# Weight loads and their two splitting operations at the highest scheduler priority, in a two-block transformer kernel on one core

## The chip, the cores and the metric

The kernel runs on one core of one Trainium2 chip. The metric is the device time of one execution in microseconds; the figure quoted is the median of several executions, and the profile is one further execution with the hardware profiler on.

## The reference

The input x has 256 tokens of 1024 features, in float32. Two blocks follow each other.

```python
def hybrid_layer(x, ...):                      # first block, two layers, l = 0 and 1
    x = x + 0.5 * swiglu(rmsnorm(x, ffn1_norm), gate, up, down)      # d_ff 2816
    h = rmsnorm(x, mix_norm) @ w_in
    o_a = chunk_relpos_attention(...)          # 6 heads, relative-position bias
    o_b = dsa_attention(...)                   # 5 heads, 64 keys chosen by an index score
    o_c = mla_attention(...)                   # 5 heads, low-rank queries and keys
    x = x + concatenate([o_a, o_b, o_c]) @ w_out
    x = x + 0.5 * swiglu(rmsnorm(x, ffn2_norm), gate, up, down)

def second_block(x, c, ctx, ...):              # one layer
    mod = silu(c) @ w_mod + b_mod              # and the same for the context
    h, hc = modulated norms of x and of ctx (256 context tokens)
    y = token_mixer(h, hc, ...)                # mLSTM and gated linear attention, both directions
    x = x + g1 * y
    x = x + g2 * peer_ffn(h2, ...)             # product-key experts, 8 heads, 16 of 16384 each
    return rms_norm(x, norm_f_g)
```

## The kernel before

All activations are kept feature-major: 128 partitions, 8 feature tiles, 256 tokens (`T`). The large products have float32 precision out of reduced-precision matmuls: each weight piece and each activation is split into a high part H (a copy in the reduced type) and a low part L (the float32 value minus H), and every product is three matmuls, H by xH, H by xL and L by xH (`mm3`, L251 to L258; `mm3t`, L260 to L267, has the weights as the moving operand). A weight is therefore ready for TensorE only when it has been loaded, copied on ScalarE (ACT) and subtracted on VectorE (DVE).

Class `W` (L205) does this in `load` (L211). A piece is up to 1024 columns of a weight. For each piece SyncE (SP) issues one DMA into a buffer `raw` (L215; five buffers), ACT copies it to `wH` (L218; three buffers), and DVE subtracts it into `wL` (L219; three buffers). Some other transfers use the same five `raw` buffers (the modulation weights at L714). `wchunk` (L248) loads a whole weight.

The order of each engine's instructions is set by a tile scheduler, which takes ready operations by priority; without other marks the priority is the order in which the program calls them. Engines run their queues in order.

The program (`run`, L1488): constants and x are loaded first, with the first four pieces of 512 columns of the first feed-forward weight (`self.ahead`) called between the four DMAs of x (L1502 to L1505). Then, for l = 0 and 1: `ffn` (L384) for ffn1, `mixer` (L494), and `ffn` for ffn2. `ffn` first calls `split_scaled` (L353: xH on ACT at L360, xL on DVE at L361) and `stats` (L284; squares on ACT at L294 and L298, sums on DVE at L299 and L300, the root by L277 to L281, the spread over partitions by two transposes at L313 and a copy `rb` on ACT at L315). Its loop over j runs 22 times: 48 matmuls into a bank `mm` (two banks while these layers run), the bank scaled by `rb` into `gu` on DVE (L400), silu on ACT (L401), the product (L403) and its split (L404, L405). During ffn2 of l = 0 and ffn1 of l = 1 the modulation of block two is computed beside (`modulation`, L714 and L717). ffn2 of l = 1 has the second block's context side beside it (`context`, L1418), with gates through exponentials on ACT (L862, L866) and on DVE (L881, L917). `mixer` projects its heads with `pair` and token-major values with `tokmajor` (the weights `win_bv` and `win_av`), and rotates with `rope` (DVE at L434, L435, L437). `latents` (L1448) then does the token mixer for x, with gates again (L863, L881, L917, L922), the running state C (L1071, L1077), the division of x by its norm (L748, eight tiles), and small matmuls on the gates' results at L954 and L962. The sums of squares before the last block's expert part are `sums` (squares on ACT, additions on DVE at L331 and L332, matmuls at L339), followed by the root and transposes at L348 (`spread`). `peer` (L1212) has the experts.

Of the kernel before, what the change touches and what calls it, by code (L numbers as in the profile page):

```python
# [9 lines left out]
F32 = mybir.dt.float32  # L10
# [5 lines left out]
AF = mybir.ActivationFunctionType  # L16
OP = mybir.AluOpType
# [187 lines left out]
class W:  # L205
# [4 lines left out]
    def load(self, pieces=None):  # L210
        k = self.k  # L211
        for o in range(self.cut * len(self.H), self.cols, self.cut)[:pieces]:
            n = min(self.cut, self.cols - o)
            raw = k.wp.tile([128, 1024], F32, name="raw", tag="raw", bufs=5)
            k.nc.sync.dma_start(raw[:, :n], self.src[:, o:o + n])  # L215
            H = k.wp.tile([128, 1024], F32R, name="wH", tag="wH", bufs=3)
            L = k.wp.tile([128, 1024], F32R, name="wL", tag="wL", bufs=3)
            k.nc.scalar.activation(H[:, :n], raw[:, :n], AF.Copy)  # L218
            k.nc.vector.tensor_tensor(L[:, :n], raw[:, :n], H[:, :n].bitcast(F32), op=OP.subtract)  # L219
            self.H.append(H)  # L220
            self.L.append(L)
        return self
# [1346 lines left out]
```

## Time and profile before

| what | value |
|---|---|
| median of 3 runs | 2152.27 us (2152.04 to 2153.51) |
| the profiled execution | 2156.47 us |
| its span, first to last instruction | 2154.5 us |
| mean granted TensorE clock, share of full | 0.991 |
| TensorE (PE) busy | 2096.3 us, 97% |
| weight loads of TensorE (PEld) busy | 2035.3 us, 94% |
| DVE busy | 1587.1 us, 74% |
| ACT busy | 1160.5 us, 54% |
| bytes moved by DMA | 385.35 MB, 179 GB/s |

The engines work side by side, so their busy times do not add up; an engine with 97% has 3% of the span in which it could still be better fed. A row of the timeline has a start, a duration, an engine, a line of the program and the operation; what stands in brackets is the idle time of the engine just before it, and what ended it. The view of waits sums such idle time by the line that waited and the operation it waited for. The clock column of a stretch is the share of full TensorE clock granted in it.

### The profile page before, as it was taken

To read this page: it belongs to the slowest core of one execution; us is meant where nothing else is said; L and a number is where in the kernel's file an instruction comes from. 1 tells how busy PE (TensorE), PEld (TensorE's weight loads), DVE (VectorE), ACT (ScalarE), POOL (GpSimd) and SP (SyncE) were. 2 spreads that over 40 slices of the span, in tenths; PEclk is the share of its full clock that TensorE was granted. 3 is DMA by queue.
4 is the path that set the end of the run, shared out by engine and by line. 5 is a ranking of instruction groups with operands and counts; after the bars stand their busy time and mean duration, and the time that the engine had idled before them with its cause. 6 is when DMAs were issued, how large, how long until landed. Compare 5 with 4: busy or idle time off the path is not lost. (4 is left out here: it accounts for less than half of the span.)

```text
span 2154.5 us, 43075 instructions
## 1 busy us (share of the span) xinstructions
PE 2096.3 (97%) x17204; PEld 2035.3 (94%) x17204; DVE 1587.1 (74%) x3211; ACT 1160.5 (54%) x2011; POOL 17.4 (1%) x35
## 2 busy tenths in 40 slices
PE   8999999999999999999999998999999999999997
PEld 8999989999999998998998798999999999999997
DVE  6776977786787697777758858888888885555555
ACT  5544465444444445547446555544588884444444
POOL 0000000000000000000000000000000000000000
PEclk9999999999999999999999999999999999999999
DMA  6666535667787753455464334555544445555553
GB/s 231 218 202 191 156 99 175 207 211 229 248 270 247 234 159 106 151 170 169 157 185 138 127 118 144 188 179 177 181 154 159 159 157 192 190 189 188 187 189 125
DMA packets 115112, 385.35 MB, mean 179 GB/s; under 512 B 12768, under 2 KB 13920, under 8 KB 114784
## 3 DMA queue, kind: packets, MB, share of 16 engines
q1 hardware_dynamic: 114912, 382.61, 54.7%
q8 instruction: 135, 2.21, 0.4%
q14 instruction: 65, 0.53, 0.1%
HBM read 380.46 MB, written 2.10 MB: 178 GB/s over the span
## 5 line engine op out<-in xcount | busy, mean ns | idle before, releaser
L219 DVE TENSOR_TENSOR wL<-raw,wH 128x1024 fp32r<-128x1024 f32 (+3 forms) x716 | 811.8, 1137 | 353.1 <-ACT wH L218 350.4
L218 ACT ACTIVATE wH<-raw 128x1024 fp32r<-128x1024 f32 (+3 forms) x716 | 705.8, 989 | 631.2 <-PE mm L257 439.0
L256 PE MATMUL mm<-xH,wH 128*128 128x256 f32 x2952 | 840.0, 285 | 9.5 <-ACT xH L360 6.4
L258 PE MATMUL mm<-xH,wL 128*128 128x256 f32 x2952 | 837.0, 284 | 8.0 <-DVE wL L219 7.9
L257 PE MATMUL mm<-xL,wH 128*128 128x256 f32 x2952 | 835.4, 283 | 1.3 <-DVE xL L361 0.8
L256 PEld LDWEIGHTS mm<-xH,wH 128*128 128x128 f32 x2952 | 559.7, 190 | 13.3 <-ACT xH L360 6.4
L258 PEld LDWEIGHTS mm<-xH,wL 128*128 128x128 f32 x2952 | 559.9, 190 | 12.3 <-DVE wL L219 11.0
L257 PEld LDWEIGHTS mm<-xL,wH 128*128 128x128 f32 x2952 | 559.9, 190 | 4.4 <-DVE xL L361 2.0
L256 PE MATMUL mm<-hl,wH 128*128 128x256 f32 x1024 | 285.8, 279 | 0.0
L257 PE MATMUL mm<-hl,wH 128*128 128x256 f32 x1024 | 285.8, 279 | 0.0
L258 PE MATMUL mm<-hl,wL 128*128 128x256 f32 x1024 | 285.8, 279 | 0.0
L258 PE MATMUL mm<-hH,wL 128*128 128x256 f32 x704 | 198.0, 281 | 6.2 <-DVE wL L219 6.1
L256 PE MATMUL mm<-hH,wH 128*128 128x256 f32 x704 | 196.6, 279 | 0.0
L257 PE MATMUL mm<-hL,wH 128*128 128x256 f32 x704 | 196.6, 279 | 0.0
L256 PEld LDWEIGHTS mm<-hl,wH 128*128 128x128 f32 x1024 | 192.4, 188 | 0.0
L258 PEld LDWEIGHTS mm<-hl,wL 128*128 128x128 f32 x1024 | 192.4, 188 | 0.0
L257 PEld LDWEIGHTS mm<-hl,wH 128*128 128x128 f32 x1024 | 192.4, 188 | 0.0
L258 PEld LDWEIGHTS mm<-hH,wL 128*128 128x128 f32 x704 | 132.1, 188 | 8.6 <-DVE wL L219 8.4
L717 DVE SCALAR_TENSOR_TENSOR prod<-raw,cv 128x1024 f32<-128x1024 f32 x64 | 78.3, 1223 | 73.8 <-DMA raw<-wmod 72.7
L257 PEld LDWEIGHTS mm<-hL,wH 128*128 128x128 f32 x704 | 132.1, 188 | 0.0
L256 PEld LDWEIGHTS mm<-hH,wH 128*128 128x128 f32 x704 | 132.0, 188 | 0.0
L401 ACT ACTIVATE gu<-gu 128x256 f32<-128x256 f32 x88 | 36.4, 414 | 105.4 <-DVE gu L400 105.1
(461 smaller groups left out, 2539.3 us busy)
## 6 DMA issues: line engine op xcount, KB each, us to landing
raw<-ffn_gu SPq DMA_DIRECT2D x174, 512.0 KB, 4.6
raw<-ut SPq DMA_DIRECT2D x128, 512.0 KB, 4.0
raw<-vt SPq DMA_DIRECT2D x128, 512.0 KB, 4.5
raw<-win SPq DMA_DIRECT2D x58, 512.0 KB, 4.4
raw<-wmod SPq DMA_DIRECT2D x48, 512.0 KB, 4.4
raw<-ffn_d SPq DMA_DIRECT2D x64, 384.0 KB, 3.2
raw<-ffn_d SPq DMA_DIRECT2D x64, 320.0 KB, 3.2
raw<-wout SPq DMA_DIRECT2D x24, 512.0 KB, 3.7
```

What stands on the lines that cost most here:

```text
L218: k.nc.scalar.activation(H[:, :n], raw[:, :n], AF.Copy)
L219: k.nc.vector.tensor_tensor(L[:, :n], raw[:, :n], H[:, :n].bitcast(F32), op=OP.subtract)
L256: mm(out, H, xH[:, k], start=first, stop=False, skip_group_check=skip)
L257: mm(out, H, xL[:, k], start=False, stop=False, skip_group_check=skip)
L258: mm(out, L, xH[:, k], start=False, stop=last, skip_group_check=skip)
L401: nc.scalar.activation(gu[:, 0], gu[:, 0], AF.Silu)
L717: nc.vector.scalar_tensor_tensor(out, raw, 1.0, cv[:, D * i:D * i + D], op0=OP.mult, op1=OP.mult, accum_out=self.mod[:, j, i:i + 1])
```

## The change

The three operations of a piece (the DMA, ACT's copy, DVE's subtraction) are put in a `high_priority()` block of the scheduler; the two tiles H and L are now named before the DMA. `high_priority()` makes the scheduler prefer these operations, on each engine, over every other one that is ready. No operation is added or removed, and buffers stay as they are. All lines behind the edit have a number that is higher by two.

```diff
             raw = k.wp.tile([128, 1024], F32, name="raw", tag="raw", bufs=5)
-            k.nc.sync.dma_start(raw[:, :n], self.src[:, o:o + n])
             H = k.wp.tile([128, 1024], F32R, name="wH", tag="wH", bufs=3)
             L = k.wp.tile([128, 1024], F32R, name="wL", tag="wL", bufs=3)
-            k.nc.scalar.activation(H[:, :n], raw[:, :n], AF.Copy)
-            k.nc.vector.tensor_tensor(L[:, :n], raw[:, :n], H[:, :n].bitcast(F32), op=OP.subtract)
+
+            with k.tc.high_priority():
+                k.nc.sync.dma_start(raw[:, :n], self.src[:, o:o + n])
+                k.nc.scalar.activation(H[:, :n], raw[:, :n], AF.Copy)
+                k.nc.vector.tensor_tensor(L[:, :n], raw[:, :n], H[:, :n].bitcast(F32), op=OP.subtract)
             self.H.append(H)
             self.L.append(L)
```

Four places show what this does to the queues. The first is the start of SP's queue, which issues the loads: `raw` are weight pieces, `cst_76` constants, `x` the input. Before:

```order
L380 DMA cst_76<-cst 128x384
L215 DMA raw<-ffn_gu 128x512
L1505 DMA x<-xT 128x512 x2
L215 DMA raw<-ffn_gu 128x512
L1505 DMA x<-xT 128x512 x2
L215 DMA raw<-ffn_gu 128x512 x2
```

and now:

```order
L219 DMA raw<-ffn_gu 128x512 x4
L219 DMA raw<-ffn_gu 128x1024
L382 DMA cst_76<-cst 128x384
L219 DMA raw<-ffn_gu 128x1024 x3
L1507 DMA x<-xT 128x512 x4
```

The four DMAs of x moved from between the first pieces to behind the eighth piece; of the last three pieces ahead of them, each needs a `raw` buffer that one of the first three pieces gives back.

The second is ACT's queue at the start, from the first piece to the first `rb`. Before:

```order
L218 ACTIVATE wH<-raw 128x512
L360 ACTIVATE xH<-x,cst_76 128x256 x2
L218 ACTIVATE wH<-raw 128x512
L360 ACTIVATE xH<-x,cst_76 128x256 x6
L294 ACTIVATE sq<-x 128x512
L298 ACTIVATE sq<-x 128x512 x2
L218 ACTIVATE wH<-raw 128x512
L298 ACTIVATE sq<-x 128x512
L218 ACTIVATE wH<-raw 128x512
L218 ACTIVATE wH<-raw 128x1024 x4
L315 ACTIVATE rb<-at 128x256
```

and now:

```order
L220 ACTIVATE wH<-raw 128x512 x3
L362 ACTIVATE xH<-x,cst_76 128x256 x8
L296 ACTIVATE sq<-x 128x512
L220 ACTIVATE wH<-raw 128x512
L300 ACTIVATE sq<-x 128x512 x2
L220 ACTIVATE wH<-raw 128x1024
L300 ACTIVATE sq<-x 128x512
L220 ACTIVATE wH<-raw 128x1024 x4
L317 ACTIVATE rb<-at 128x256
```

The copy of the ninth piece, which stood behind `rb`, now stands ahead of it, as the last of the nine.

The third is DVE's queue in `latents`, from the division of x (L748 before, L750 now) to the gates (`la`, `lf`). Before:

```order
L748 SCALAR_TENSOR_TENSOR x<-x,cst_76,rb 128x256 x8
L1071 TENSOR_SCALAR wv<-mv,col_12316 128x129 x3
...
L1077 SCALAR_TENSOR_TENSOR C<-C,abc_12314,c 128x129 x2
L863 TENSOR_SCALAR la<-at,cst_11262 128x256 x2
L872 MEMSET mv 128x8
L219 TENSOR_TENSOR wL<-raw,wH 128x1024
L863 TENSOR_SCALAR la<-at,cst_11262 128x256
L219 TENSOR_TENSOR wL<-raw,wH 128x1024 x2
L881 SCALAR_TENSOR_TENSOR lf<-G,E 64x256
```

and now:

```order
L750 SCALAR_TENSOR_TENSOR x<-x,cst_76,rb 128x256 x4
L221 TENSOR_TENSOR wL<-raw,wH 128x1024
L750 SCALAR_TENSOR_TENSOR x<-x,cst_76,rb 128x256 x4
L221 TENSOR_TENSOR wL<-raw,wH 128x1024 x2
L1079 SCALAR_TENSOR_TENSOR C<-C,abc_12314,c 128x129
L1073 TENSOR_SCALAR wv<-mv,col_12316 128x129 x3
...
L865 TENSOR_SCALAR la<-at,cst_11262 128x256
L221 TENSOR_TENSOR wL<-raw,wH 128x1024
L883 SCALAR_TENSOR_TENSOR lf<-G,E 64x256
L919 TENSOR_TENSOR la<-la,E 128x1024
```

The three subtractions that stood behind all of the state's updates now stand inside and right behind the division of x.

The fourth is DVE's queue at the sums of squares ahead of the expert part (`x` is the last update of the residual, `sq` the squares). Before:

```order
L331 TENSOR_TENSOR sq<-sq 128x256
L1482 SCALAR_TENSOR_TENSOR x<-c,mod,x 128x256 x2
L332 TENSOR_TENSOR sq<-sq 128x256
L219 TENSOR_TENSOR wL<-raw,wH 128x1024
L757 TENSOR_SCALAR rm<-at 128x2
```

and now:

```order
L1484 SCALAR_TENSOR_TENSOR x<-c,mod,x 128x256 x2
L333 TENSOR_TENSOR sq<-sq 128x256
L221 TENSOR_TENSOR wL<-raw,wH 128x1024
L333 TENSOR_TENSOR sq<-sq 128x256
L334 TENSOR_TENSOR sq<-sq 128x256
```

The subtraction moved from behind the last addition to ahead of the last two, and two additions moved behind the last update of x.

## Rows read from the trace of the kernel before

**Rows 1.** The page, busy time of the engines.

```profile
PE 2096.3 (97%) x17204; PEld 2035.3 (94%) x17204; DVE 1587.1 (74%) x3211; ACT 1160.5 (54%) x2011; POOL 17.4 (1%) x35
```

**Rows 2.** Waits of PE, whole span: us in total, times, longest.

```profile
PE mm L258 <- DVE wL L219: 14.0, 21, 2.3
...
PE mm L266 <- DVE wL L219: 6.1, 3, 3.4
...
PE c L266 <- DVE wL L219: 1.5, 1, 1.5
...
PE c L258 <- DVE wL L219: 0.7, 1, 0.7
```

**Rows 3.** Timeline of PE, matmuls 1 to 48: start, us, operation, [idle before].

```profile
6.37 0.58 PE L256 MATMUL mm<-xH,wH 128*128 128x256 f32 x1 [6.37 <-ACT xH L360]
...
11.84 0.41 PE L258 MATMUL mm<-xH,wL 128*128 128x256 f32 x1
12.05 0.41 PE L256 MATMUL mm<-xH,wH 128*128 128x256 f32 x1
...
16.91 0.28 PE L257 MATMUL mm<-xL,wH 128*128 128x256 f32 x1
17.02 0.28 PE L258 MATMUL mm<-xH,wL 128*128 128x256 f32 x1
```

**Rows 4.** Waits of PE from 400 to 760 us.

```profile
PE mm L258 <- DVE wL L219: 8.9, 17, 1.4
```

**Rows 5.** Timeline of PE in the first mixer, at the values' weight.

```profile
218.34 0.42 PE L266 MATMUL mm<-wL,xH 128*128 128x328 f32 x1 [1.39 <-DVE wL L219]
```

**Rows 6.** Waits of PE from 960 to 1000 us.

```profile
PE mm L258 <- DVE wL L219: 2.3, 1, 2.3
...
PE mm L256 <- ACT wH L218: 0.9, 1, 0.9
```

**Rows 7.** Timeline of PE in latents: the two long waits, and the gates' matmul.

```profile
1175.36 0.39 PE L258 MATMUL mm<-xH,wL 128*128 128x256 f32 x1 [1.80 <-DVE wL L219]
...
1189.05 0.50 PE L266 MATMUL mm<-wL,xH 128*128 128x512 f32 x1 [3.37 <-DVE wL L219]
...
1201.51 0.48 PE L954 MATMUL at<-dg,ones 64*128 64x128 f32 x2
```

**Rows 8.** Stretches of 2 us: busy us of PE, PEld, DVE, ACT, POOL; granted clock; DMA.

```profile
982.00:984.00 2.00, 0.51 (x5) 0.30 (x3) 1.94 (x5) 1.99 (x3) 0.00 (x0) 1.00 0.07 27
984.00:986.00 2.00, 1.17 (x7) 1.17 (x8) 2.00 (x4) 1.13 (x3) 0.00 (x0) 0.81 0.10 25
986.00:988.00 2.00, 2.00 (x11) 2.00 (x11) 1.83 (x7) 1.21 (x2) 0.00 (x0) 0.50 0.63 231
988.00:990.00 2.00, 2.00 (x15) 1.91 (x15) 2.00 (x5) 0.81 (x1) 0.00 (x0) 0.84 0.06 14
```

**Rows 9.** DMA, 0 to 40 us: rate per us, and issues (KB each, median us to landing).

```profile
GB/s 0 60 254 129 367 358 215 238 334 383 420 418 426 250 41 266 262 340 274 274 328 258 246 311 209 250 94 213 262 156 283 152 115 279 139 90 295 160 164 307
...
x<-xT SPq DMA_DIRECT2D x4, 256.0 KB, 5.1
```

**Rows 10.** Timeline of ACT at the start.

```profile
5.81 0.91 ACT L360 ACTIVATE xH<-x,cst 128x256 fp32r<-128x256 f32 x2
...
20.06 1.06 ACT L218 ACTIVATE wH<-raw 128x1024 fp32r<-128x1024 f32 x1 [1.77 <-PE mm L257]
```

**Rows 11.** Timeline of DVE around the first use of rb.

```profile
21.33 1.22 DVE L219 TENSOR_TENSOR wL<-raw,wH 128x1024 fp32r<-128x1024 f32 x1
22.47 0.68 DVE L400 TENSOR_TENSOR gu<-mm,rb 128x512 f32<-128x512 f32 x1
```

**Rows 12.** Stretch of 40 us in the second mixer, columns as in rows 8.

```profile
760.00:800.00 40.00, 38.44 (x284) 35.56 (x283) 37.92 (x101) 20.57 (x33) 1.30 (x1) 1.00 0.54 168
```

**Rows 13.** Timeline of DVE in latents, at the end of the gates' chain.

```profile
1195.25 0.41 DVE L948 TENSOR_TENSOR gd<-b,mu 64x256 f32<-64x256 f32 x1
```

**Rows 14.** Timeline of PE at the sums of squares.

```profile
1322.12 1.75 PE L339 MATMUL at<-ones,sq 128*128 128x1 f32 x12 [1.72 <-DVE sq L332]
```

## Prediction

> **What bounds the kernel now.** First the busy times [rows 1]: TensorE (PE) works 2096.3 us of a span of 2154.5, so all its idle time is 58.2 us. DVE, which makes every wL, is at 74%, so only the order of its work, not its amount, can starve PE. Then PE's waits [rows 2]: what it waits for the second splitting operation sums to 14.0 + 6.1 + 1.5 + 0.7 = 22.3 us. That is the most that a better order of weights can win directly. The single longest wait, 6.37 us, is for the first xH, and that is no weight [rows 3]: before the first matmul PE needs a piece and x. So the same priority that can shorten 22.3 us can lengthen 6.37.
>
> Where the 22.3 us lie decides. 8.9 of them fall between 400 and 760 us [rows 4], where the modulation of the second block shares `raw`, and DVE, with the feed-forward layers; the new order of all queues there is the old one, so I count nothing. The others: 1.39 us at `win_bv` in the first mixer [rows 5] and as much in the second, 2.3 + 1.5 + 0.7 and 0.9 for a wH around 980 us [rows 2, 6], and 1.80 + 3.37 in `latents` [rows 7].
>
> An idle PE also costs clock. In the 2.0 us in which PE was busy 0.51, the granted clock still stood at 1.00; then it read 0.81, 0.50 and 0.84 in the next three stretches [rows 8], between the levels 2.4 and 1.2 GHz. Lost there: 0.19 x 1.17 + 0.50 x 2 + 0.16 x 2, about 1.5 us. I take 1.7 us as the price of one idle stretch of about 2 us, between 0 (a short idle) and 3.6 us (4 us of idle and of half clock twice as long).
>
> **The start: a cost.** x's DMAs took 5.1 us from issue to landing when one or two pieces stood ahead [rows 9]; now x lies behind eight pieces and the constants. Ahead of the end of x's first quarter stand 4 x 256 + 4 x 512 + 192 + 256 KB = 3520 KB, 3.60 MB. The first 12 us of the rate row move 3.18 MB, the first 13 move 3.60 [rows 9]. So x's first quarter lands near 13.0 us where xH started at 5.81 [rows 10]. The first matmul came 0.56 us behind that, at 6.37 [rows 3]; it now comes near 13.65. If the queue never falls below some 400 KB per us it is 12.6; if the last three pieces wait longer for their `raw` buffers, 14.6.
>
> By the Trainium skill, DMA: Bandwidth & Descriptors, section Queues, rings and completion order, each engine takes the descriptors of a queue in ring order, so x would not overtake the pieces. The same page puts the HBM side at about 358 GB/s and the port side at 435, an estimate of 8.3 to 10.1 us for 3.60 MB; the rate row reaches 426 but averages less, so the row's 13 us are kept.
>
> From there PE runs without waits for pieces, all of which are ready. The matmuls started 0.21 us apart until 12.05, and 0.11 to 0.12 us apart at 16.91 [rows 3]: the lower level of the clock for about 6 us, or 28 matmuls. With the same here, 48 matmuls take 28 x 0.214 + 20 x 0.118 = 8.4 us, to 22.0 us; before, the 48th started at 17.02 and ended its share at 17.1. **Cost 4.9 us**, from 3.6 to 6.0.
>
> Then a new wait. ACT's copy of the ninth piece now stands ahead of `rb`, and it needs a wH buffer that the sixth piece holds until the 96th matmul is done (the old row shows such a copy waiting 1.77 us for PE [rows 10]). Behind it comes the subtraction of the ninth piece on DVE, and behind that the first `gu`, which frees the bank that matmul 97 needs, since there are two. From the end of matmul 96: copy 1.06 [rows 10], subtraction 1.22, gu 0.68 [rows 11], together 2.96, of which some 0.25 is overlap. **Cost 2.7 us**, from 0 (if a wH buffer is free sooner) to 4.0 (with the transposes ahead). After such an idle stretch the clock falls: **1.7 us**, 0 to 3.6. Together the start costs 9.3 us, 5 to 12.
>
> **The mixers: a small gain.** At `win_bv` the subtraction moves ahead of the rotation's DVE work, and the waits of 1.39 go: **2.8 us won** [rows 5], 0 to 2.8. What was covering it, the masked copies behind the rotation, now end later by two subtractions, about 1.6 us, against the 1.4 that PE gains; the matmuls on them had no wait, so this is about even. In the head part the values' matmuls come earlier as filler, and fewer are left between the later heads, while DVE there is the busier engine (37.92 of 40 us in the second mixer [rows 12]). I charge **1 us** for both mixers; bounds 0 to 5.
>
> **960 to 1000 us: a gain.** The subtractions move ahead of the context's splits and products. Of 2.3 + 0.9 + 1.5 + 0.7 = 5.4 us about 1.3 stay, since one subtraction still stands behind `lf` (L881) and `la` (L917), which wait for ACT. So 4.1 direct, and of the two falls of the clock behind these waits a bit more than one, 1.9. **6.0 won**, 3 to 8.
>
> **Latents: a gain given back in part.** Three subtractions move from behind the state's updates to inside the division of x, and later ones ahead of the scans: the waits of 1.80 and 3.37 go [rows 7], and two falls of the clock with them, 3.4. Against that the gates' chain (`lf`, scans, `mu`, `it`) stands behind five subtractions of 1.22, some on its path. The matmul at L954 that takes its result came at 1201.51 [rows 7]; the last DVE step of the chain ended at 1195.66 [rows 13], and with ACT's exponential behind it the inputs were ready some 4 us before. PE now reaches it 8.6 us earlier and 47 matmuls (7 us) later in its order, but the chain is some 6 us later: a new wait of about 3 us, and a fall of 1.7 behind it. **3.9 won**, 1 to 8.
>
> **The sums of squares: a cost.** PE waits 1.72 us there for the last addition [rows 14]. One subtraction (1.22) and two more additions (0.33 each as they follow each other) now stand between the last update of x and that addition: **1.9 us**, 0 to 2.5. PE has nothing else to do there.
>
> In the expert part PE has no wait that a weight ends, and the swaps there are of single operations: 0, from nothing won to 2 lost.
>
> **Sum:** 9.3 - 2.8 + 1.0 - 6.0 - 3.9 + 1.9 = -0.5 us. The profiled execution took 2156.47 us, 2.0 more than its span and 4.2 more than the median of the runs; the terms are differences against that span, so I set the sum against the median: 2152.27 - 0.5, about **2152 us**. A measurement of this kernel can tell about 0.2%, 4.3 us, from no change; this is inside.
>
> **Rivals.** *Weights win* (faster): the start costs 6.6, because the first `gu` is not held up, and latents and the stretch around 980 give 7 and 7.5. Then 6.6 - 2.8 + 1 - 7.5 - 7 + 1.9 = -7.8, 2144.5 us. For it: ACT is at 54% and DVE has slack in these stretches. Against it: two queues show the ninth piece ahead of the first `rb` and `gu`.
>
> *The gates' chain and the heads are starved* (slower): each subtraction that overtakes a step of a chain on which PE waits next costs its 1.22 us. It decides once five or more stand on the path to L954 and two or more on that of each mixer's last heads: latents then win nothing (3.9 lost), each mixer costs 2.4 (4.8 less the 1 counted), so -0.5 + 3.9 + 3.8 = +7.2, 2159.5 us. For it: DVE at 37.92 of 40 us [rows 12]. Against it: in these stretches PE's own matmuls are still long enough to hide several microseconds.
>
> *The order hardly changes where it counts*: in the layers between 400 and 760 us this is so already; if also the moves around 980 and in latents bring only the direct half (3 and 1 won), the start remains: 9.3 - 2.8 + 1 - 3 - 1 + 1.9 = +5.4, 2157.7 us.
>
> **How the numbers follow.** Forecast 0.38; weights win 0.29; starved 0.20; only the start remains 0.13. So faster by over 0.2%: 0.29, within: 0.38, slower: 0.33. The range reaches from a little below the first rival to a little above the second: 2143 to 2161. The forecast's own range is 2148 to 2156.5.
>
> **What the changed profile should show.** First matmul near 13.7 us, 48th near 22.0; PE idle near 27.5 us for about 2.7, then matmuls 0.21 us apart; no wait at `win_bv`; at most 1.5 us of wL waits from 960 to 1000; a wait of some 3 us at L954 or L962 (two lines later now) near 1190; the wait at L339 grown from 1.72 to about 3.6; and the 8.9 us between 400 and 760 as they were. If the first matmul comes before 10 us, or if waits on DVE results other than wL grow by more than 5 us in the mixers, I am wrong in mechanism and not in size.

## The result, and the profile after

The changed kernel takes 2164.41 us (median of 6 runs, 2161.41 to 2165.75), the kernel before in the same session 2152.15 us (6 runs, 2149.70 to 2156.09). The ratio is 1.0055, with a 95% interval from 1.0044 to 1.0066: 11.8 us slower, 9.5 to 14.2 (the two medians differ by 12.3). The profiled execution has a span of 2162.9 us, 8.4 more than that of before, whose own execution lay 4.3 us over its median.

The busy time of the engines on the page of the changed kernel, which answers to [rows 1]:

```profile
PE 2099.3 (97%) x17204; PEld 2036.5 (94%) x17204; DVE 1588.2 (73%) x3211; ACT 1161.5 (54%) x2011; POOL 17.7 (1%) x35
```

The same instructions, and the same busy times within 3 us. What changed is when PE is idle, and at which clock it works. PE's waits, which answer to [rows 2] (lines are two higher):

```profile
PE mm L258 <- ACT xH L362: 16.6, 1, 16.6
PE mm L260 <- DVE wL L221: 8.1, 15, 1.3
PE at L341 <- DVE sq L334: 6.2, 3, 3.4
...
PE at L956 <- DVE dg L939: 4.1, 1, 4.1
PE mm L258 <- DVE gu L402: 1.9, 1, 1.9
```

The change does what it says: the waits for wL fell from 22.3 us in all to 8.1, and of these 8.1 all but 1.7 lie between 400 and 780 us, where nothing was expected to move (6.4 us now, 8.9 before and 8.3 in a second profile of the kernel before). The wait for the first xH grew from 6.37 to 16.62 us. Two long waits are new: the matmul on the gates' result (L956), and the first `gu` (L402).

Where along the program the time went is best seen by the same instruction in both traces. The table has the end of nine DVE instructions on the two timelines, in us:

| instruction (line of before) | before | after | shift |
|---|---|---|---|
| copy of the first root (L310) | 21.39 | 31.24 | +9.85 |
| an update of x by ffn1, layer 0 (L416) | 192.00 | 204.63 | +12.63 |
| first update of x by mixer 0 (L699) | 341.57 | 355.04 | +13.47 |
| last listed update of x ahead of mixer 1 (L416) | 743.94 | 752.47 | +8.53 |
| copy of a root behind mixer 1 (L310) | 903.27 | 911.53 | +8.26 |
| an update of x by ffn2, layer 1 (L416) | 1086.01 | 1084.41 | -1.60 |
| a short convolution in latents (L790) | 1241.45 | 1244.09 | +2.64 |
| last sum of squares before the experts (L332) | 1321.97 | 1327.65 | +5.68 |
| last sum of squares of the program (L332) | 2143.42 | 2151.81 | +8.39 |

So some 12 us are lost at the start, about 10 won between 900 and 1090 us, and 4, 3 and 3 lost in latents, at the sums of squares and in the expert part. The fall by 5 us between 341 and 744 us is not a gain of the change, as the runs below show.

### The profile page after: what moved, and what is told of

Read it like the earlier page. It is cut to its first block, busy times and chain, and to the rows that moved or that the text cites. A ratio compares the mean times of both kernels' runs of the same rounds, so it can differ in the third digit from the quotient of the medians.

```text
span 2162.9 us, 43093 instructions
## 1 busy us (share of the span) xinstructions
PE 2099.3 (97%) x17204; PEld 2036.5 (94%) x17204; DVE 1588.2 (73%) x3211; ACT 1161.5 (54%) x2011; POOL 17.7 (1%) x35
```

## The experiments

Nearly all of them restrict the high priority to parts of the program. `stage` is set where the parts begin: `start` (the first weight and the first four loops of ffn1 in layer 0), `ffn`, `mix`, `ctx` (ffn2 of layer 1 with the context side and the norm behind it), `lat`, `peer`:

```diff
+HOT = ("ctx", )
...
-            with k.tc.high_priority():
+            with k.tc.high_priority() if k.stage in HOT else nullcontext():
```

Ratios are to the kernel before on the same chip; its medians lay between 2153.8 and 2155.3 us. The microseconds beside a ratio are worked out from it. The plain differences of the medians are up to 2.4 us off: 10.5 instead of 12.3 for `only_start`, 7.1 instead of 9.5 for `only_lat`, 0.4 instead of 2.4 for `all_but_start`.

### The start

`only_start` has HOT = ("start", ).

> High priority only for the pieces of the first weight and of the first four loops of the first feed-forward layer; all later pieces as before. Theory A (the cost is made at the start and nothing behind it takes it back): first matmul near 16.6 us, and 11.5 to 12.5 us slower than before. Rival B (the shift against before fell from 12 to 8 us between 400 and 760 us, so the delay is partly caught up behind weights that come early): first matmul near 16.6 us all the same, but only 7 to 9 us slower.

Measured: 1.0057 [1.0044, 1.0070], 12.3 us slower. Theory A holds and B falls: the delay is taken whole to the end. In this trace the shift does not fall between the table's rows at 341 and 744 us, it rises by 2.2, and in that of `all_but_start` by 1.8; a second profile of the kernel before is 2.2 us shorter there than the first. That stretch differs by some microseconds from execution to execution with the order unchanged, and no run shows a gain in it.

How the 12 us come about, in the trace of the changed kernel. SP's own timeline (start, duration of the issuing, operation):

```profile
0.73 2.28 SPq L219 DMA_DIRECT2D raw<-ffn_gu  x5
3.06 0.43 SPq L382 DMA_DIRECT2D cst<-cst  x1
5.89 1.82 SPq L219 DMA_DIRECT2D raw<-ffn_gu  x3
7.76 3.15 SPq L1507 DMA_DIRECT2D x<-xT  x4
```

SP stood from 3.49 to 5.89, until the first piece was split and gave its buffer back; x stood behind it. The DMA view of the first 40 us, which answers to [rows 9]:

```profile
GB/s 0 31 147 297 389 346 364 312 198 168 152 332 404 385 401 297 127 41 0 0 0 0 229 246 57 229 303 143 246 332 254 246 279 98 217 250 33 0 0 0
...
x<-xT SPq DMA_DIRECT2D x4, 256.0 KB, 8.3
```

After 8 us the rate falls to 150 to 200 for three microseconds: the first five pieces were through, and the next transfers had been issued late. And x took 8.3 us instead of 5.1. Issue and time to landing of the eighth piece and of the first and last quarter of x:

```profile
7.39 0.33 SPq L219 DMA_DIRECT2D raw<-ffn_gu  x1
7.76 0.42 SPq L1507 DMA_DIRECT2D x<-xT  x1
...
10.25 0.66 SPq L1507 DMA_DIRECT2D x<-xT  x1
```

```profile
raw<-ffn_gu SPq DMA_DIRECT2D x1, 512.0 KB, 8.0
x<-xT SPq DMA_DIRECT2D x1, 256.0 KB, 8.3
...
x<-xT SPq DMA_DIRECT2D x1, 256.0 KB, 7.7
```

So they landed one by one, the piece at 15.4 us, x's first quarter at 16.04 and its last at 18.0. The rate row runs ahead of the landings: by 16 us it has 4.22 MB (its first 16 numbers), where the pieces, the constants and one quarter of x make 3.60. It reaches 3.60 at 14.2 us. On PE, which answers to [rows 3], with the 48th matmul and the 97th:

```profile
16.62 0.58 PE L258 MATMUL mm<-xH,wH 128*128 128x256 f32 x1 [16.62 <-ACT xH L362]
...
24.27 0.28 PE L260 MATMUL mm<-xH,wL 128*128 128x256 f32 x1
...
33.66 0.36 PE L258 MATMUL mm<-xH,wH 128*128 128x256 f32 x1 [1.93 <-DVE gu L402]
```

The 48th matmul is 7.25 us late, the 97th waits 1.93 us for its bank, and the clock is half behind that (columns as in [rows 8]):

```profile
34.00:36.00 2.00, 2.00 (x14) 2.00 (x13) 1.63 (x5) 1.16 (x3) 0.00 (x0) 0.59 0.65 233
36.00:38.00 2.00, 2.00 (x12) 2.00 (x12) 0.00 (x0) 0.00 (x0) 0.00 (x0) 0.55 0.04 16
```

That is 2 x 0.41 + 2 x 0.45, or 1.7 us. PE's wait for the transposes ahead of it grew by 0.5 (0.61 us, 0.12 before): 7.25 + 0.5 + 1.93 + 1.7 = 11.4 us.

By the Trainium skill, DMA: Bandwidth & Descriptors, section Queues, rings and completion order, each DMA engine takes a queue's descriptors in ring order. The trace agrees: x's quarters landed behind the last piece. The estimate from that page's rates, 8.3 to 10.1 us, was still further from the 16.04 us than the row's 13.0.

`start_x_hot` tells x from the rest. It is `only_start` with the DMAs of x, and of the first constants, at high priority too:

```diff
-                self.load_consts(self.sp, 0)
+                with tc.high_priority():
+                    self.load_consts(self.sp, 0)
...
-                    nc.sync.dma_start(self.x[:, k:k + 2], self.ap["xT"][:, T * k:T * k + 2 * T])
+                    with tc.high_priority():
+                        nc.sync.dma_start(self.x[:, k:k + 2], self.ap["xT"][:, T * k:T * k + 2 * T])
```

> As only_start, but the DMAs of x and of the first constants have the high priority too, so that they go out ahead of the pieces again. Theory A (nearly all of the start's cost is the late x): first matmul back to 6 to 8 us, the wait of 1.9 us for the first gu stays, since the copy of the ninth piece still stands ahead of rb; 1 to 4 us slower than before. Rival B (the cost is the pieces' copies and subtractions in ACT's and DVE's queues, x or not): still 8 us or more slower.

Measured: 1.0014 [1.0004, 1.0023], 3.0 us slower. PE's timeline in this run, at the first matmul, the 48th and the 97th:

```profile
8.93 0.58 PE L262 MATMUL mm<-xH,wH 128*128 128x256 f32 x1 [8.93 <-ACT wH L223]
...
16.55 0.28 PE L264 MATMUL mm<-xH,wL 128*128 128x256 f32 x1
...
26.26 0.36 PE L262 MATMUL mm<-xH,wH 128*128 128x256 f32 x1 [1.69 <-DVE gu L408]
```

The first matmul came at 8.93, not at 6 to 8: it now waits for the first piece, since three of x's four DMAs go out ahead of it. But 9 of the 12 us are gone with the place of x (and of the constants, which moved with it). The 48th matmul is no later than before, 16.55 us against 17.02, so what is left lies behind it: the bank's wait stayed, 1.69 us, as theory A had it.

`start_dma_only` gives the priority at the start to the DMA alone:

```diff
             with k.tc.high_priority() if k.stage in HOT else nullcontext():
                 k.nc.sync.dma_start(raw[:, :n], self.src[:, o:o + n])
-                k.nc.scalar.activation(H[:, :n], raw[:, :n], AF.Copy)
-                k.nc.vector.tensor_tensor(L[:, :n], raw[:, :n], H[:, :n].bitcast(F32), op=OP.subtract)
+            k.nc.scalar.activation(H[:, :n], raw[:, :n], AF.Copy)
+            k.nc.vector.tensor_tensor(L[:, :n], raw[:, :n], H[:, :n].bitcast(F32), op=OP.subtract)
```

> As only_start, but only the DMA of a piece has the high priority, its copy and its subtraction not. Theory A (the place of x behind eight pieces in SP's queue is the cost, and the bank's wait behind the ninth piece follows from the late x): first matmul near 16.6 us and 10 to 13 us slower than before, as only_start. Rival B (the copies and subtractions make it): under 5 us slower.

Measured: 1.0050 [1.0036, 1.0064], 10.8 us slower; first matmul at 15.63 us. With `start_x_hot` this settles the start: the order of SP's queue is the cost. What the priority of the two splitting operations adds to it, 12.3 - 10.8 = 1.5 us, is not to be told from nothing, with intervals of 3 us either way.

`all_but_start` leaves the start as it was.

> High priority everywhere but at the start (those pieces as before). Theory A: first matmul at 6.4 us as before; what is left is the gain of some 8 us around 980 us against losses in latents, at the sums of squares and in the expert part: within 2 us of before. Rival B: some 4 to 5 us faster than before, since the stretch from 400 to 760 us would bring its 5 us as well.

Measured: 1.0011 [0.9999, 1.0024], 2.4 us slower, at the edge of theory A; rival B's 4 us of gain are not there. Its executions are far apart, from 2147.8 to 2161.1 us; a likely reason stands under latents.

### The context's stage

`only_ctx` has HOT = ("ctx", ).

> High priority only while the second feed-forward of the second layer and the context side are programmed (some 890 to 1050 us). Theory A: the shift there, -8 us, stands alone: 6 to 9 us faster than before, about 2144 us, and no half clock from 984 to 1000 us. Rival C (the gain there is only made because work from the rest is pulled ahead of it): under 3 us.

Measured: 0.9969 [0.9959, 0.9979], 6.7 us faster, 2147.20 us: the gain stands alone, and rival C falls. PE's waits in the changed kernel from 940 to 1050 us, which answer to [rows 6], and the stretch from 960 to 1000 us:

```profile
PE mm L260 <- DVE wL L221: 1.3, 1, 1.3
...
PE c L267 <- DVE mk L793: 0.6, 1, 0.6
```

```profile
960.00:1000.00 40.00, 37.94 (x280) 35.26 (x279) 33.12 (x62) 28.31 (x43) 0.00 (x0) 1.00 0.51 166
```

Of 5.4 us of waits 1.3 stayed, a single wait for wL, and the clock stood at 1.00. A new one of 0.6 came. The trace of `only_ctx` reads the same (1.3, 0.6 and 1.00). In the first profile of the kernel before, and in a second one, `before_again`, the same stretch reads:

```profile
960.00:1000.00 40.00, 34.48 (x232) 31.73 (x231) 31.49 (x61) 28.11 (x41) 0.00 (x0) 0.91 0.45 142
```

```profile
960.00:1000.00 40.00, 34.49 (x223) 31.22 (x222) 30.26 (x59) 28.97 (x45) 0.00 (x0) 0.91 0.48 157
```

`before_again` is the kernel before, unchanged.

> The kernel before, unchanged, for a second profile of it. The first profile took 2156.5 us, 4 us over the median. Theory H (that execution alone lost some 4 us around 980 us, where the traces of only_start and only_lat, whose code there is that of before, are 4.4 us shorter): the second profile is 4 us shorter in just that stretch. Rival: the two profiles agree there within 1 us.

Measured: one execution of 2153.78 us, and a stretch around 980 us like the first one's (0.91 both times, [rows 8] is from there). So theory H falls as it was put. But `only_start` has the same code there and the same four waits, and in the same place, moved by its 12 us:

```profile
972.00:1012.00 40.00, 33.19 (x236) 30.14 (x235) 30.95 (x61) 30.03 (x46) 0.00 (x0) 1.00 0.51 159
```

The clock did not fall (a fifth wait for wL, of 1.3 us, shows instead), and 4.4 us were saved. Ten traces of the study have this code unchanged: the clock fell in seven of them and not in `only_start`, `only_lat` and `start_x_hot`. So whether waits of 1.5 to 2.3 us cost clock was not the same in all executions. The gain of the context is 8.7 us where the clock had fallen (`only_ctx` against `before_again`, from 930 to 1010 us), 4.1 where it had not (against `only_start`), and 6.7 by the ratio.

### Latents

`only_lat` has HOT = ("lat", ).

> High priority only in latents. Theory A (the gates' chain is overtaken by subtractions, PE idles some 4 us at the matmul on its result, and then runs some 20 us at half clock): 3 to 6 us slower than before, with the wait and the half clock in the trace. Rival D (the wait there comes from what was pulled ahead before, in the context): the two wL waits of 1.8 and 3.4 us go, no new wait, and 5 to 8 us faster.

Measured: 1.0044 [1.0031, 1.0057], 9.5 us slower, more than theory A's 3 to 6. The two wL waits of 1.80 and 3.37 are gone, as in the whole change. What came in their place, on PE's timeline of the changed kernel, answers to the last of [rows 7]:

```profile
1199.87 0.79 PE L956 MATMUL at<-dg,ones 64*128 64x128 f32 x2 [4.07 <-DVE dg L939]
```

and behind it, in stretches of 2 us:

```profile
1198.00:1200.00 2.00, 0.13 (x1) 0.13 (x1) 1.97 (x5) 1.93 (x8) 0.00 (x0) 0.58 0.54 190
1200.00:1202.00 2.00, 2.00 (x11) 1.66 (x11) 1.78 (x7) 2.00 (x4) 0.00 (x0) 0.50 0.52 164
...
1216.00:1218.00 2.00, 2.00 (x11) 2.00 (x11) 0.00 (x0) 0.00 (x0) 0.00 (x0) 0.50 0.03 12
1218.00:1220.00 2.00, 2.00 (x10) 1.53 (x10) 0.00 (x0) 0.90 (x1) 0.00 (x0) 0.80 0.00 0
```

All stretches between these two pairs read 0.50: PE has 19 us of work at half clock, 9 us lost, though it is never idle. The clock stood at half for 20.5 us. In `all_but_start` the same wait, 4.08 us, ended at 1193.72, and the clock came back after 6.8 us:

```profile
1192.00:1194.00 2.00, 0.28 (x2) 0.28 (x3) 2.00 (x5) 1.93 (x8) 0.00 (x0) 1.00 0.47 158
1194.00:1196.00 2.00, 2.00 (x12) 1.44 (x11) 2.00 (x7) 2.00 (x4) 0.00 (x0) 0.63 0.63 180
1196.00:1198.00 2.00, 2.00 (x9) 1.62 (x8) 1.04 (x1) 1.39 (x3) 0.00 (x0) 0.50 0.20 82
1198.00:1200.00 2.00, 2.00 (x10) 1.66 (x9) 0.99 (x3) 0.00 (x0) 0.00 (x0) 0.50 0.73 238
1200.00:1202.00 2.00, 2.00 (x11) 1.73 (x10) 0.95 (x4) 1.06 (x1) 0.00 (x0) 0.66 0.06 25
1202.00:1204.00 2.00, 2.00 (x12) 1.33 (x10) 1.64 (x5) 0.81 (x1) 0.00 (x0) 1.00 0.03 8
```

The same wait in the same code cost 3.4 us of clock in this execution and 9.5 in the other. Three more traces have this wait, 4.07 or 4.08 us long, and in all three the clock stood at half for 20.5 us. Here are `only_lat`, `all_but_ctx` and `all_but_peer`, 20 us from the end of the wait on:

```profile
1196.00:1216.00 20.00, 19.43 (x69) 15.06 (x70) 10.41 (x27) 8.34 (x14) 0.00 (x0) 0.51 0.21 67
```

```profile
1212.00:1232.00 20.00, 19.51 (x69) 15.14 (x70) 10.32 (x27) 8.35 (x14) 0.00 (x0) 0.51 0.21 68
```

```profile
1204.00:1224.00 20.00, 18.70 (x67) 14.56 (x68) 11.13 (x27) 8.97 (x15) 0.00 (x0) 0.50 0.23 77
```

The same 80 matmuls follow the wait in all five traces, in the same order. So what PE has to do behind the wait does not alone decide the length. One thing differs: in the four the clock fell 1.3 to 1.6 us before PE started again (the 0.58 of 1198 to 1200 us above), in the fifth 0.8 us after. Whether that decides was not tried. The two lengths fit the scatter of `all_but_start`: of its 12 executions five had a mean clock of 0.988 or 0.989 and a median of 2159.7 us, seven one of 0.991 to 0.993 and 2153.7. That is 6.0 us apart, as much as 9.5 and 3.4.

The Trainium skill, TensorE: Matmul & The Clock Gate, section What's actually happening, says of the start of a kernel that the number of slow matmuls varies from run to run, and that one should not fit to a specific count. The traces here show the like behind a wait within the kernel, with 6.8 us in one and 20.5 in four.

`lat_gates` puts the gates' exponentials, scans and small operations of latents at high priority too:

```diff
-        nc.vector.scalar_tensor_tensor(lf, G[64:], 0.0, E[64:, 4], op0=OP.min, op1=OP.subtract)
+        with self.tc.high_priority() if lat else nullcontext():
+            nc.vector.scalar_tensor_tensor(lf, G[64:], 0.0, E[64:, 4], op0=OP.min, op1=OP.subtract)
...
```

> As only_lat, but the gates' exponentials, scans and their small operations in latents have the high priority too, so that subtractions of pieces no longer overtake them. Theory A (the overtaken gates' chain makes the wait of 4.1 us at the matmul on its result, and the half clock behind it): the wait is under 1 us and no half clock from 1198 to 1219 us; the two wL waits stay away or are under 2 us together; 4 to 9 us faster than before. Rival E (PE comes to that matmul too early whatever the chain does, since its own order moved): a wait of 3 us or more stays, and 3 us or more slower than before.

Measured: 1.0001 [0.9987, 1.0015]. PE's waits from 1160 to 1240 us in this run:

```profile
PE mm L272 <- DVE wL L224: 2.1, 1, 2.1
PE at L968 <- DVE dg L951: 1.2, 1, 1.2
```

Rival E falls: the wait of 4.1 shrank to 1.2 and the loss of 9.5 us with it, so the overtaken chain was its cause. Theory A's gain did not come: a wL wait of 2.1 us is back. In this trace DVE did not serve both in time: what the chain won the pieces lost.

### The mixers and the expert part

`only_mix` has HOT = ("mix", ).

> High priority only in the two mixers. Theory A (by the shift of landmarks the two waits of 1.4 us at win_bv go and about as much comes back between the heads): within 3 us of before. Rival F (DVE, the busiest engine there, starves the heads): 4 us or more slower. Rival G (the wait at win_bv goes and nothing comes back): 3 us faster.

Measured: 0.9999 [0.9988, 1.0009]. The wait of 1.39 us at `win_bv` ([rows 5]) is gone from the trace of this run, and its longest waits between 200 and 350 us are new ones:

```profile
PE o L477 <- ACT et L476: 0.6, 1, 0.6
PE mm L262 <- ACT av L675: 0.6, 1, 0.6
```

A few waits of 0.2 to 0.6 us between the heads take the place of the one of 1.39. Theory A holds.

`only_peer` has HOT = ("peer", ).

> High priority only in the expert part. Theory A (by the shift of landmarks that part is 2.7 us longer with the change, in small gaps between 1660 and 1790 us, and the sums of squares lose nothing to it): 1.5 to 4 us slower than before. Rival I (the loss in that part comes from elsewhere): within 1 us of before.

Measured: 1.0020 [1.0011, 1.0030], 4.3 us slower. Theory A had its size about right (up to 4), and its place half wrong: the sums of squares lose to these pieces as well. PE's wait there, which answers to [rows 14], in this run:

```profile
PE at L345 <- DVE sq L338: 3.0, 1, 3.0
```

In the whole change it is 3.4. But `only_lat` and `all_but_peer`, which have no priority in the expert part, show 3.0 as well: latents' own pieces lengthen this wait too, and its 1.3 us stand in the cost of both parts.

In the whole change a fall of the clock ahead of that wait adds to it. It cost some 1.5 us. It is in all four traces with the 20.5 us and in neither profile of the kernel before:

```profile
1310.00:1312.00 2.00, 1.73 (x7) 1.05 (x6) 2.00 (x5) 0.42 (x1) 0.00 (x0) 0.74 0.58 184
1312.00:1314.00 2.00, 1.99 (x10) 1.93 (x10) 1.80 (x6) 0.87 (x3) 0.00 (x0) 0.50 0.56 176
```

In `only_peer` the shift against the second profile of before rises by 2.9 us at the sums of squares (the wait, and a half clock behind it that lasted 3.4 us longer) and by another 2.8 between 1660 and 1800 us, where a stretch of PE reads, here and in that second profile of before:

```profile
1680.00:1720.00 40.00, 39.56 (x372) 38.75 (x370) 34.39 (x60) 31.62 (x88) 0.00 (x0) 1.00 0.48 159
```

```profile
1680.00:1720.00 40.00, 40.00 (x387) 39.73 (x386) 34.50 (x61) 32.26 (x90) 0.00 (x0) 1.00 0.48 159
```

15 matmuls fewer in 40 us at full clock: many gaps too small to stand as waits. Which swapped operation makes them was not tried.

### Do the parts add up?

Alone they sum to 12.3 - 6.7 + 9.5 + 0 + 4.3 = +19.4 us; the whole costs 11.8. (By the plain differences of the medians it is 14.6 and 12.3, so how much does not add is uncertain.) Two combinations and three omissions tell which part does not add. `ctx_lat_gates` has HOT = ("ctx", "lat", ) and the gates' chain as in `lat_gates`; `all_but_start_lat` has HOT = ("ffn", "mix", "ctx", "peer", ); the other three leave out the part of their name.

> High priority in the context's stage and in latents, with the gates' chain of latents at the same priority: the parts that won or came out even. Theory A (places add up): 6 to 9 us faster than before, about as only_ctx. Rival J (with the context out of the way the gates' chain comes in time, and both waits of latents are won too): 11 us or more faster.

Measured: 0.9967 [0.9954, 0.9981], 7.1 us faster: no more than the context alone, rival J falls.

> The change without the start and without latents. Theory A (places add up: context -7, mixers 0, expert part +2.7): 3 to 6 us faster than before. Rival J2 (what the context wins is only moved into latents, where PE then waits as long): within 2 us of before.

Measured: 0.9994 [0.9983, 1.0004], 1.3 us faster, 3.7 faster to 0.9 slower: less than theory A, whose lower end it does not exclude, and inside rival J2's bound. The parts alone give -6.7 + 0 + 4.3 = -2.4, so J2's reason is not needed for it; `only_ctx`, where 6.7 us were won ahead of unchanged latents, speaks against it.

> The whole change without latents. Theory K (latents cost less in company than alone, as the step from all_but_start_lat to all_but_start says, 3.7 us): the change without it is 1 to 5 us faster than with it, that is 7 to 11 us slower than before. Rival L (its cost alone, 9.5 us, holds in the whole change too): within 4 us of before.

Measured: 1.0039 [1.0026, 1.0052], 8.4 us slower: latents cost 3.4 us in the whole change, theory K.

> The whole change without the context's stage. Theory K (latents lose the same or less when the context does not come early): the 6.7 us that the context alone wins are missing, 16 to 20 us slower than before. Rival M (what the context wins in the whole change is smaller, since PE then waits in latents for what it gained): 11 to 14 us slower, as the whole change.

Measured: 1.0090 [1.0077, 1.0103], 19.4 us slower: the context wins 7.6 in the whole, so rival M falls.

> The whole change without the expert part. Theory K (the expert part's cost, 4.3 us alone, adds to the rest): 6 to 9 us slower than before. Rival N (the sums of squares lose as much to latents' own pieces, so that part's cost is not additive): 10 us or more slower.

Measured: 1.0038 [1.0024, 1.0052], 8.2 us slower, 5.2 to 11.2: by the middle the expert part costs 3.6, but the interval reaches into rival N's range, and N's reason is seen in the trace, where the wait at the sums of squares is 3.0 us all the same. N is not excluded.

So the start, the context and the expert part keep their size in company, within the error (12.3 alone and 11.8 - 2.4 = 9.4 in the whole for the start, with intervals of 2 to 3 us each); the mixers were not left out. Latents seem not to: 9.5 alone, 3.4 to 3.7 with the context ahead of them. The 1.3 us of the sums of squares, which two parts share, explain some of that. The two lengths of the half clock may explain more, if the short one came less often in `only_lat`; with its five executions that is not shown, and the profiled execution of the whole change has the long one.

The fastest kernel of the study is one with the priority in the context's stage alone: 2147.20 us against 2154.03, ratio 0.9969. `ctx_lat_gates`, at 2145.65 us against 2153.84, is not to be told from it.

## Why the prediction was wrong

The forecast was no measurable change, 2152 us, with 2143 to 2161; the time is 2164.41. The likeliest case was an even balance of a cost at the start and gains behind it. One of the gains was a cost, another was none, and the costs came out as forecast or larger. Term by term, in us:

| term | forecast | its own run | in the whole change |
|---|---|---|---|
| start | +9.3 (5 to 12) | +12.3 | +9.4 |
| mixers | -1.8 | -0.2 | not run |
| 960 to 1000 us | -6.0 (3 to 8 won) | -6.7 | -7.6 |
| latents | -3.9 (1 to 8 won) | +9.5 | +3.4 |
| sums of squares and expert part | +1.9 | +4.3 | +3.6 |
| 400 to 760 us | 0 | not run | order unchanged |

The last column sums to 8.8; the 3 us that are left to 11.8 lie within the error of its terms.

**The start** was right in mechanism, step by step: x late, the 97th matmul waiting for its bank behind the ninth piece, the clock falling behind that. The term mis-sized is "x's first quarter lands near 13.0 us": it landed at 16.04. The step took the rate of the old order: in the new one SP waited for a buffer, the rate fell to 150 to 200 GB/s for three microseconds, and 3.60 MB had moved at 14.2 us. And it took bytes in the rate row for bytes landed, which is another 1.8 us. The trace of before shows this lag too: x's first quarter, issued at 1.65 and landed 4.1 us later, came about 1 us after the row [rows 9] had the 0.72 MB up to its end. The upper bound for the first matmul, 14.6 us, named the wait for the buffer but was too low. The half clock lasted 17 matmuls and not 28, which gave some of it back. The bank's wait (2.7 forecast, 0.5 and 1.93 measured) and the clock behind it (1.7, and 1.7) were right. The rows of before for that lag, issue and time to landing:

```profile
1.65 0.42 SPq L1505 DMA_DIRECT2D x<-xT  x1
```

```profile
x<-xT SPq DMA_DIRECT2D x1, 256.0 KB, 4.1
```

**960 to 1000 us** was right in waits (4.1 of 5.4 gone, 1.3 left, as forecast). That the sum came out too has some luck in it: the clock's share, 1.9 forecast, is all or nothing by the traces, and the ratio is a mean over such executions. **The mixers** were right as far as the wait goes; what came back was 1.6 larger than charged, within the error of the run.

**Latents** is the step that failed. "Two falls of the clock with them, 3.4" and "a new wait of about 3 us, and a fall of 1.7 behind it": the two waits went, and the new one came where it was said, at the matmul on the gates' result, with 4.07 us. But a fall of the clock was priced at 1.7 us from [rows 8], where the clock was back after 4 us. Behind L956 it stood at half for 20.5 us in four of five traces, and 6.8 in the fifth. That price, 9.5 us, was above the bound of 3.6 that was given. In the trace of the changed kernel the terms are -5.2 (waits) - 3.4 (clock) + 4.1 + 9.5 = +5.0, where the table shows a shift of 4.2. Why the same wait had two lengths of half clock behind it stays open.

**The sums of squares** came out as forecast in kind, the wait growing from 1.72 to 3.4 (3.6 was forecast); the fall of the clock ahead of it was not foreseen. **The expert part** was put at nothing, "0 to 2 lost", because no row of waits was there; the loss of 2.8 us is in gaps that the view of waits does not show.

Of the rivals, *starved* was nearest in sign and in place (latents' chain), with 2159.5 us. It had latents lose what they win, but took the start at its forecast size and left the heads in; the heads did not starve.

## What to carry to other kernels

Giving all weight loads the highest priority moves them ahead of whatever else is short of time, and here that was the input itself, the chain of gates and the sum of squares that PE waits for next: some 12 us of waits outside 400 to 780 us were won and more was lost. Give the priority to a stretch in which the trace shows PE waiting for a weight and in which the overtaken work is not what PE waits for next: both the context and latents had such waits, and only the context won. Take the input of the kernel out of it. When a wait is moved to another place, do not price the clock behind it by one fall elsewhere: here one and the same wait cost 3.4 us of clock in one trace and 9.5 in four, so the price is a range that holds both.

## What was not expected of the hardware

After one idle stretch of 4.1 us the granted clock stood at half for 6.8 us in one execution and for 20.5 us in four others, with PE busy all the time on the same matmuls. Around 980 us the same waits brought the mean clock of 40 us to 0.91 in both profiles of the kernel before and left it at 1.00 in `only_start`. Four DMAs issued one behind the other in one queue, behind eight others, landed in order and 0.6 to 0.7 us apart, but 1.8 us later than the bytes in the rate row would have it.
